# Layer 1 of a two-layer diffusion backbone: some tiles of the neighbourhood attention move to a pool at the other end of SBUF

## The chip, the core and the metric

One NeuronCore of a Trainium2 chip runs the whole kernel in one launch. Its engines are TensorE (PE; its weight loads are listed as PEld), VectorE (DVE), ScalarE (ACT), GpSimd (POOL) and SyncE (SP), which here only issues DMAs. The metric is the device time of one execution in microseconds, lower is better; it is quoted as the median of several runs. A profile is one further execution, taken by the hardware profiler.

## The reference

Two layers work on 1024 latent tokens and 256 context tokens of width 1024. Layer 0 is two kinds of grouped attention. Layer 1, which the change touches, has a convolution branch and a neighbourhood attention over a 16 by 64 grid, in which every query sees the 256 context tokens and a window of 8 by 16 grid places with a bias from a table:

```python
def odd_mixer(h_lat, h_ctx, w_in, w_out, dw_w, dw_b, ln_g, ln_b, rpb, update_ctx):
    ...
    cv, cgl, cg, dq, dk, dv, dg = split_cols(h_lat @ w_in, ODD_WIDTHS)
    x_cv, x_cgl, x_cg, x_dq, x_dk, x_dv, x_dg = split_cols(h_ctx @ w_in, ODD_WIDTHS)
    ...
    oc = conformer_conv(cv, cgl, cg, dw_w, dw_b, ln_g, ln_b)
    ...
    def d_row(args):
        r, qr = args
        rs = jnp.clip(r - kh // 2, 0, rows - kh)
        kr = lax.dynamic_slice_in_dim(k_grid, rs, kh, axis=1).reshape(bsz, kh * GRID_W, D_HEADS, HEAD_DIM)
        ...
        bias = rpb[:, dr_idx][:, :, dc_idx] + col_mask[None, None]
        ...
        return gqa_attend(qr[:, :, :, None, :], kk, vv, bias).reshape(bsz, GRID_W, D_W)
    ...
    y_lat = jnp.concatenate([oc, od * jax.nn.silu(dg)], axis=-1) @ w_out
```

`conformer_conv` is a convolution over 31 tokens in each channel, a layer norm, a SiLU and a gate; `gqa_attend` is a softmax of the scaled and biased scores times the values. All is float32.

## The kernel before

**Precision.** Every product of two float32 operands is made of three matmuls (L334 to L336) on a high and a low part: `split` (L312) rounds to the high part on ScalarE (L314, a cast) and subtracts on VectorE or GpSimd (L317) for the low part. Names ending in h or H are high, those in l or L low.

**Scheduling.** The program is written out step by step, and a scheduler that simulates the engines at build time decides the order in which each engine, and each DMA queue, gets its instructions. Tiles come from pools. A pool that opens where a closed pool lay makes each of its tiles wait for the last users of the old tiles in the same bytes (`reuse_waits="tile"`). Nearly all DMAs are issued from SP, in order: one that waits holds those behind it.

**Layer 1 in order.** Pool `cu` holds uc and gc, the convolution's output and gate (two tiles of 128 x 4 x 1024). Pool `cv` (L1224) holds the convolution's tiles; in it run the convolution's projections, its 31 taps on VectorE, ScalarE and GpSimd, and `d_proj(0)`, the attention's projections for heads 0 and 1. Then pool `ln` (L1244) holds the tiles of the layer norm, which runs in two halves of 512 tokens (`ln_steps`, L1124 to L1143: VectorE for the most part, with stores of Oc at L1143) beside `d_proj(1)`. Then `cu` closes, and two pools open: `d0` (L1261) with yo and the probability tiles ph, pl, pf, and `d1` (L1265) with the keys, values and bias tables. The attention's main loop then runs woven with `d_proj(2)`, `d_proj(3)` and the output projection.

**d_proj(i)** computes queries, keys, values and gates of two heads as sums over eight pieces of the contraction (its weights come in four loads, wr, cast to wh and wl), splits them (spq L1153 and L1155, spk, spv) and stores them in DRAM as QD, KD, VD and GD. In the order rows below, p_2723 and p_2736 are the query projections of `d_proj(2)` for the two halves of the tokens, p_2756 and p_2790 its key projections.

**The attention** works in 16 groups, one for each head and half of the grid's columns. A group needs:
- KA: the high and low part of the head's keys, 64 partitions each, loaded by L391 and L392 (two buffers), and KB, a copy of the high part by ScalarE (L397) with four rows of ones by GpSimd (L386).
- QH and QL, the queries, in pool `kv1`, loaded long before.
- a row maximum for each of four blocks of 128 queries (`maxes`, L1318): matmuls of QH with KA into the banks mx (L1326 for the context, two blocks in a bank; L1334 for the window, 440 or 320 keys), reduced by VectorE (L1328; L1335 adds the bias table bm on the way and takes an accumulator read as a second instruction). bm is loaded by L1293, three tables in a group, into two buffers.
- nmt (L418), its transpose trn (L439) and from it the last rows of QL (L440).
- for each of seven tiles: scores st (L511 from KA and QH, L515 from KB and QL), the bias bs added by VectorE (L520; loaded by L1303), the exponential (L521, L523), its split ph and pl, and the product with the values (L462 to L464; V is loaded by L1316 and has ones set by L381).

The banks mx are two, so a maximum's matmul waits for the reduction of the one two before it. The first two groups are prepared ahead of the first tile. A step of the fill (`d_proj(2)`) is held behind the sixth last L511, so the fill cannot run far ahead of the attention.

Of the kernel before, what the change touches and what calls it, by code (L numbers as in the profile page):

```python
# [10 lines left out]
F32 = mybir.dt.float32  # L11
F32R = mybir.dt.float32r
# [6 lines left out]
P = 128  # L19
# [16 lines left out]
BMB = 2  # L36
# [52 lines left out]
def tile_kernel(ctx: ExitStack, tc: tile.TileContext, a, out):  # L89
# [22 lines left out]
    def nm(s):  # L112
        uid[0] += 1
        return f"{s}_{uid[0]}"
# [263 lines left out]
    def v_tiles(pool, n, bufs=1):  # L378
        Vs[:] = [pool.tile([P, n, 192], F32R, tag="V", name=nm("Vt"), bufs=bufs) for _ in range(bufs)]
        for V in Vs:  # L380
            GP.memset(V[:, :, 128:192].bitcast(F32), 1.0)  # L381

    def k_tiles(pool, n, bufs=1):
        KB = pool.tile([P, n * P], F32R, tag="KB", name=nm("KBt"), bufs=bufs)
        KA = pool.tile([P, n * P], F32R, tag="KA", name=nm("KAt"), bufs=bufs)
        GP.memset(KB[64:68, :].bitcast(F32), 1.0)  # L386
        Ks.append((KA, KB))

# [645 lines left out]
    with ExitStack() as l1x:  # L1034
# [189 lines left out]
        with tc.tile_pool(name="cv", bufs=1, reuse_waits="tile") as vp:  # L1224
            stg[0] = vp
            taps = const("taps", [P, 4, 31], SY, vp)
            Us = []

            def convs():
                for i in range(4):  # L1230
                    while len(Us) <= i:
                        yield
                    yield from conv_steps(vp, i, Us[i])
            bg = convs()
            for i in range(4):
                U = vp.tile([P, NLAT + 30], F32, tag="U", name=nm("U"), bufs=4)
                for _ in conv_proj(vp, i, U):
                    pump(2)
                Us.append(U)
            for _ in d_proj(0):  # L1240
                pump(1)
            for _ in bg:
                pass
        with tc.tile_pool(name="ln", bufs=1, reuse_waits="tile") as vp:  # L1244
            stg[0] = vp
            lnbh = vp.tile([P, 4], F32, tag="lnbh", name="lnbh")
            VE.tensor_scalar(lnbh, lnb, 0.5, None, op0=ALU.mult)
            ones5 = vp.tile([P, P], F32, tag="ones5", name="ones5")
            VE.memset(ones5, 1.0 / 512.0)

            def lns():
                for c in range(2):
                    yield from ln_steps(vp, c)
            bg = lns()
            for _ in d_proj(1):
                pump(1)
            for _ in bg:
                pass
# [5 lines left out]
        dlow.tile([P, 48], F32, tag="pad", name="pad")  # L1264
        dpool = l1x.enter_context(tc.tile_pool(name="d1", bufs=1, reuse_waits="tile"))  # L1265
        for _ in range(2):
            k_tiles(dpool, 12, 2)
        v_tiles(dpool, 7, 2)
        od = [None, None]

        def load_head(hd):
# [4 lines left out]
        def group1(gi, hd, hf):  # L1276
            i, e = divmod(hd, 2)
            ds = slice(e * 64, (e + 1) * 64)
            bms, bss = {}, {}
# [9 lines left out]

            def load_bm(b):  # L1290
                n = (KROWS[b][1] - KROWS[b][0]) * NW
                bms[b] = dpool.tile([P, 440], F32, tag="bm", name=nm("bm"), bufs=BMB)[:, :n]
                SY.dma_start(bms[b], a["d_bm"][hd, hf, :, BMO[b] : BMO[b] + n])  # L1293
                if b == 1:
                    bms[2] = bms[1]

            def ahead(t):
                if g.tiles[t][3] is not None:
                    n = g.tiles[t][2]
                    t -= 1  # L1300
                    w = dpool.tile([P, 512 if n > 352 else 352], F32, tag="bsl" if n > 352 else "bss", name=nm("bs"),
                                   bufs=1 if n > 352 else 4)
                    SY.dma_start(w[:, :n], a["d_bs"][hd, hf, :, BSO[t] : BSO[t] + n])  # L1303
                    bss[t] = w[:, :n]
# [324 lines left out]
```

## Time and profile before

| | |
|---|---|
| time, three runs | 1554.67 us median, 1553.38 to 1559.51 |
| profiled execution, its own time | 1557.54 us |
| its span (first to last instruction) | 1555.8 us |
| mean granted TensorE clock | 0.959 of full speed |
| mean DMA traffic over the span | 128 GB/s |

Three kinds of rows are shown. A row of the timeline has the start in us from the span's start, the length in us, engine, line, operation, out<-in, and the number of instructions merged; in brackets stands how long the engine was idle before it, and what it waited for. A row of stretches has start and end, the length, the busy time of PE, PEld, DVE, ACT and POOL (with instruction counts), the granted TensorE clock as a share of full speed, the mean share in which the 16 DMA engines were busy, and GB/s. A row of the chain of waits has start, length and what held the end at that time. A row of DMA issues has out<-in, the queue, the count, KB each and the median us from issue to landing. Matmuls are pipelined: a 128 x 512 one is listed with about 0.39 us, while the next starts 0.23 us later.

### The profile page before, as it was taken

The page shows a single profiled execution, that of the slowest core. Times are in us where ns is not written, and L with a number is a line of the kernel's source. Part 1 is how long each engine was busy: PE and PEld are TensorE (multiplying, and loading weights), DVE is VectorE, ACT ScalarE, POOL GpSimd, SP SyncE. Part 2 cuts the span into 40 slices and gives each one's busy share as a digit, 9 for nine tenths or more (in the row PEclk, how much of TensorE's full clock was granted, in tenths as well). Part 3 has the DMA queues.
Part 4 walks back from the last instruction along what each step waited for, and adds up shares of the span by engine and source line. Part 5 has one row for each costly group of instructions (what it writes and reads, how often), then busy time and mean ns, then how long its engine had stood idle before and what let it go on. Part 6 is the DMA issues. An engine that isn't in the chain of part 4 may idle for free.

```text
span 1555.8 us, 21467 instructions
## 1 busy us (share of the span) xinstructions
PE 1462.5 (94%) x7084; PEld 1177.6 (76%) x7084; DVE 1046.0 (67%) x2113; ACT 747.6 (48%) x1418; POOL 800.2 (51%) x637
## 2 busy tenths in 40 slices
PE   6899999998998999999999889999999799989995
PEld 2776888896896778886877568888887688878874
DVE  2832466579678855567677848999756566577766
ACT  3721434444434564447656565443434455455562
POOL 3430334446455766557646665665632334364674
PEclk7899999999999999999999799999999899999996
DMA  9474315423312245121202021211446777877632
GB/s 365 150 247 136 102 61 174 149 65 98 114 55 77 86 145 196 45 79 43 58 28 80 23 65 60 60 48 41 152 158 212 208 220 234 257 231 230 191 86 108
DMA packets 154168, 199.83 MB, mean 128 GB/s; under 512 B 14716, under 2 KB 95816, under 8 KB 154056
## 3 DMA queue, kind: packets, MB, share of 16 engines
q1 hardware_dynamic: 147392, 186.88, 38.0%
q10 hardware_dynamic: 6664, 11.57, 2.2%
q8 instruction: 56, 0.92, 0.3%
q14 instruction: 56, 0.46, 0.1%
HBM read 148.07 MB, written 49.02 MB: 127 GB/s over the span
## 4 chain that ended last, share of the span: by engine, by line
PE 81%; DVE 11%; DMA 3%; issue 2%; ACT 2%; POOL 1%; SPq 0%; DVEq 0%; POOLq 0%; ACTq 0%
PE p L334 7%; PE p L336 7%; PE p L335 7%; PE ov L462 5%; PE ov L464 5%; PE ov L463 4%; PE st L511 4%; PE st L515 4%; PE po L334 4%; PE po L335 4%; PE po L336 4%; PE pq L334 3%; PE pq L335 3%; PE pq L336 3%; PE pg L334 2%
## 5 line engine op out<-in xcount | busy, mean ns | idle before, releaser
L317 POOL TENSOR_TENSOR pl<-pf,ph 128x512 fp32r<-128x512 f32 (+4 forms) x321 | 395.6, 1243 | 381.8 <-ACT ph L314 332.8
L523 ACT ACTIVATE pf<-st 128x512 f32<-128x512 f32 x284 | 166.2, 596 | 214.0 <-PE st L515 175.6
L317 POOL TENSOR_TENSOR wl<-wr,wh 128x512 fp32r<-128x512 f32 (+2 forms) x131 | 170.4, 1312 | 138.6 <-ACT wh L314 123.7
L314 ACT CAST ph<-pf 128x512 fp32r<-128x512 f32 (+4 forms) x364 | 209.3, 588 | 28.4 <-PE ov L463 16.3
L334 PE MATMUL p<-hh,wh 128*128 128x512 f32 x448 | 176.7, 395 | 3.0 <-DVE spv L317 1.4
L335 PE MATMUL p<-hl,wh 128*128 128x512 f32 x448 | 174.3, 390 | 0.0
L336 PE MATMUL p<-hh,wl 128*128 128x512 f32 x448 | 172.3, 390 | 0.0
L511 PE MATMUL st<-QH,KAt 128*128 128x512 f32 (+4 forms) x364 | 142.0, 391 | 7.5 <-ACT pf L523 6.7
L462 PE MATMUL ov<-ph,Vt 128*128 128x512 f32 (+4 forms) x364 | 143.3, 394 | 3.1 <-DVE y L672 2.0
L464 PE MATMUL ov<-pl,Vt 128*128 128x512 f32 (+4 forms) x364 | 142.4, 391 | 2.1 <-POOL pl L317 2.0
L463 PE MATMUL ov<-ph,Vt 128*64 128x512 f32 (+4 forms) x364 | 141.0, 387 | 0.0
L515 PE MATMUL st<-QL,KBt 68*128 68x512 f32 (+4 forms) x364 | 137.3, 388 | 2.0 <-DVE QL L440 1.9
L1099 DVE SCALAR_TENSOR_TENSOR cps<-U,taps,cps 128x512 f32<-128x512 f32 x184 | 126.0, 752 | 0.7
L314 ACT CAST wh<-wr 128x512 fp32r<-128x512 f32 (+2 forms) x134 | 81.0, 613 | 91.4 <-DMA wr<-in_od_d_dram 18.4
L334 PEld LDWEIGHTS p<-hh,wh 128*128 128x128 f32 x448 | 84.2, 188 | 21.8 <-ACT wh L314 1.9
L635 DVE TENSOR_REDUCE mp<-mx 128x1 f32<-128x512 f32 x128 | 85.3, 682 | 19.4 <-PE mx L634 18.5
L336 PEld LDWEIGHTS p<-hh,wl 128*128 128x128 f32 x448 | 84.2, 188 | 17.5
L335 PEld LDWEIGHTS p<-hl,wh 128*128 128x128 f32 x448 | 84.2, 188 | 16.8 <-issue 0.5
L334 PE MATMUL pq<-wh,hh 128*128 128x384 f32 x256 | 88.0, 344 | 2.8 <-ACT hh L314 2.8
L511 PEld LDWEIGHTS st<-QH,KAt 128*128 128x128 f32 x364 | 70.1, 193 | 24.9 <-ACT pf L523 9.9
L464 PEld LDWEIGHTS ov<-pl,Vt 128*128 128x128 f32 x364 | 71.0, 195 | 23.3 <-POOL pl L317 5.0
L956 DVE SCALAR_TENSOR_TENSOR x<-po,modT,x 128x512 f32<-128x512 f32 (+1 forms) x72 | 47.0, 658 | 61.0 <-PE po L336 60.5
(280 smaller groups left out, 3491.9 us busy)
## 6 DMA issues: line engine op xcount, KB each, us to landing
mw<-in_mod_w_dram SPq DMA_DIRECT2D x16, 1024.0 KB, 5.4
Q<-qs SPq DMA_DIRECT2D x40, 256.0 KB, 2.1
QH<-Q SPq DMA_DIRECT2D x80, 128.0 KB, 2.7
mw<-in_mod_w_dram SPq DMA_DIRECT2D x16, 512.0 KB, 6.9
wr<-in_od_d_dram SPq DMA_DIRECT2D x32, 256.0 KB, 3.1
wr<-in_ev_qkv_dram SPq DMA_DIRECT2D x16, 384.0 KB, 5.2
KAt<-KD SPq DMA_DIRECT2D x16, 384.0 KB, 5.9
wr<-in_od_wo_dram SPq DMA_DIRECT2D x22, 256.0 KB, 3.2
```

The lines of the kernel that those rows point to most:

```text
L314: acts.append(SC.copy(hi, src))
L317: (GP if leng == "g" else VE).tensor_tensor(lo, src, hi.bitcast(F32), op=ALU.subtract)
L334: PE.matmul(o, lh, rh, start=first, stop=False)
L335: PE.matmul(o, lh, rl, start=False, stop=False)
L336: last.append(PE.matmul(o, ll, rh, start=False, stop=end))
L462: PE.matmul(o, V[:, 64:192], ph[:, :n], start=(t == 0), stop=False)
L463: PE.matmul(g.ov[0:64, q0 : q0 + n], V[:, 0:64], ph[:, :n], start=False, stop=False)
L464: PE.matmul(o, V[:, 64:192], pl[:, :n], start=False, stop=(last and g.sink is None))
L511: sts.append(PE.matmul(st[:, :n], KA[:, cs], g.QH[:, q0 : q0 + n], start=True, stop=False))
L515: PE.matmul(st[:, :n], KB[0:68, cs], g.QL[0:68, q0 : q0 + n], start=False, stop=True)
L523: acts.append(SC.activation(pf[:, :n], st[:, :n], AF.Exp, scale=1.0 if g.bias else SCALE))
L1099: VE.scalar_tensor_tensor(pc, uc, w, pc, op0=ALU.mult, op1=ALU.add)
```

## The change

A pool `dh` is opened from the other end of SBUF (`side="right"`) right behind the convolution's pool, ahead of the layer norm's. The tiles KA, V, bm and bs, with the same sizes and numbers of buffers as before, are allocated in it instead of in `d1`. KB stays in `d1`, and no instruction is added or taken away.

```diff
@@ -380,9 +380,9 @@
-    def k_tiles(pool, n, bufs=1):
+    def k_tiles(pool, hi, n, bufs=1):
         KB = pool.tile([P, n * P], F32R, tag="KB", name=nm("KBt"), bufs=bufs)
-        KA = pool.tile([P, n * P], F32R, tag="KA", name=nm("KAt"), bufs=bufs)
+        KA = hi.tile([P, n * P], F32R, tag="KA", name=nm("KAt"), bufs=bufs)
@@ -1241,6 +1241,7 @@
             for _ in bg:
                 pass
+        dhi = l1x.enter_context(tc.tile_pool(name="dh", bufs=1, side="right", reuse_waits="tile"))
         with tc.tile_pool(name="ln", bufs=1, reuse_waits="tile") as vp:
@@ -1264,8 +1265,8 @@
         for _ in range(2):
-            k_tiles(dpool, 12, 2)
-        v_tiles(dpool, 7, 2)
+            k_tiles(dpool, dhi, 12, 2)
+        v_tiles(dhi, 7, 2)
@@ -1289,7 +1290,7 @@
-                bms[b] = dpool.tile([P, 440], F32, tag="bm", name=nm("bm"), bufs=BMB)[:, :n]
+                bms[b] = dhi.tile([P, 440], F32, tag="bm", name=nm("bm"), bufs=BMB)[:, :n]
@@ -1298,7 +1299,7 @@
-                    w = dpool.tile([P, 512 if n > 352 else 352], F32, tag="bsl" if n > 352 else "bss", name=nm("bs"),
+                    w = dhi.tile([P, 512 if n > 352 else 352], F32, tag="bsl" if n > 352 else "bss", name=nm("bs"),
```

Lines behind the new one have a number higher by one in the changed kernel (L1293 becomes L1294). With other waits the scheduler puts the instructions in another order, from the start of `d_proj(1)` on. Three places follow.

**SP's queue.** Before, at the end of the layer norm: stores of its output Oc and of the queries QD, and between them the loads of head 0's keys, of bm and of bs.

```order
L1143 DMA Oc<-uc 128x512 x2
L391 DMA KAt_11659<-KD_9572 64x1536
L1143 DMA Oc<-uc 128x512
L392 DMA KAt_11659<-KD_9572 64x1536
L1143 DMA Oc<-uc 128x512
L1159 DMA QD_9570<-spq_11769 128x2x256
L1293 DMA bm_11685<-in_d_bm_dram 128x440
L1159 DMA QD_9570<-spq_11769 128x2x256
L1293 DMA bm_11687<-in_d_bm_dram 128x320
L1303 DMA bs_11827<-in_d_bs_dram 128x256
```

After, these loads stand among the gate and value stores of `d_proj(0)`, ahead of the layer norm; the weights of `d_proj(1)` (its third and fourth piece) follow a few rows later, behind one more L392.

```order
L1217 DMA VD_9576<-spv_10996 128x512 x2
L391 DMA KAt_11662<-KD_9572 64x1536
L392 DMA KAt_11662<-KD_9572 64x1536
L1294 DMA bm_11688<-in_d_bm_dram 128x440
L1294 DMA bm_11690<-in_d_bm_dram 128x320
L1304 DMA bs_11830<-in_d_bs_dram 128x256
L1304 DMA bs_11832<-in_d_bs_dram 128x352
L1304 DMA bs_11834<-in_d_bs_dram 128x512
L391 DMA KAt_11665<-KD_9572 64x1536
L1198 DMA GD_9580<-sgd_11037 256x1x256
L1217 DMA VD_9576<-spv_11076 128x768
```

What moved: two of the three bm tables of group 0, three of its bs tables and three of the four halves of the keys of heads 0 and 1 went ahead by a whole `d_proj`.

**TensorE, between the key projection and the first scores.** mx_2725 to mx_2730 are the maxima of group 0, mx_2738 to mx_2743 those of group 1. Before:

```order
L336 MATMUL p_2790_11972<-hh_9483,wl_11711 128x512
L1334 MATMUL mx_2729_11755<-KAt_11659,QH_11670 128x320
L1334 MATMUL mx_2730_11758<-KAt_11659,QH_11670 128x320
L1326 MATMUL mx_2738_11792<-KAt_11659,QH_11675 128x256 x2
L1334 MATMUL mx_2739_11796<-KAt_11659,QH_11675 128x440
L1334 MATMUL mx_2740_11799<-KAt_11659,QH_11675 128x440
L1326 MATMUL mx_2741_11802<-KAt_11659,QH_11675 128x256 x2
L1334 MATMUL mx_2742_11815<-KAt_11659,QH_11675 128x320
L1334 MATMUL mx_2743_11818<-KAt_11659,QH_11675 128x320
L439 MATMUL trn_11823<-ident,nmt_11761 4x128
L515 MATMUL st_11842<-QL_11671,KBt_11658 128x512
```

After:

```order
L334 MATMUL p_2790_11975<-hh_9483,wh_11713 128x512
L1335 MATMUL mx_2740_11802<-KAt_11662,QH_11678 128x440
L335 MATMUL p_2790_11975<-hl_9484,wh_11713 128x512
L1327 MATMUL mx_2741_11805<-KAt_11662,QH_11678 128x256 x2
L336 MATMUL p_2790_11975<-hh_9483,wl_11714 128x512
L1335 MATMUL mx_2742_11818<-KAt_11662,QH_11678 128x320
L1335 MATMUL mx_2743_11821<-KAt_11662,QH_11678 128x320
L439 MATMUL trn_11826<-ident,nmt_11764 4x128
L515 MATMUL st_11845<-QL_11674,KBt_11661 128x512
L515 MATMUL st_11878<-QL_11674,KBt_11661 128x256
L439 MATMUL trn_11867<-ident,nmt_11824 4x128
```

What moved: behind the key projection's last matmul stand two maxima instead of eight. All of group 0's maxima now stand ahead of the key projections (mx_2725 to mx_2728 at the start of the query projections, mx_2729 and mx_2730 at their end), mx_2738 and mx_2739 between p_2756 and p_2790.

**VectorE, the second half of the layer norm.** uc is scaled (L1137), shifted (L1140), gated (L1141, L1142); spv and spq are splits of `d_proj(1)` and `d_proj(2)`. Before:

```order
L1137 SCALAR_TENSOR_TENSOR uc<-uc,lng,s_2667_11420 128x512 x4
L1140 TENSOR_SCALAR uc<-uc,lnb 128x512
L317 TENSOR_TENSOR spv_11636<-trv_11633,spv_11636 128x4x64
L1140 TENSOR_SCALAR uc<-uc,lnb 128x512
L1141 SCALAR_TENSOR_TENSOR uc<-thl_11602,uc 128x512
```

After:

```order
L1329 TENSOR_REDUCE mp_11734<-mx_2725_11735 128x2
L1336 ISA mx_2726_11739,mp_11734<-mx_2726_11739,bm_11688 128x440
L1336 ISA mp_11734 128x1
L1137 SCALAR_TENSOR_TENSOR uc<-uc,lng,s_2667_11423 128x512 x4
L317 TENSOR_TENSOR spv_11639<-trv_11636,spv_11639 128x4x64
L1336 ISA mx_2727_11751,mp_11734<-mx_2727_11751,bm_11688 128x440
L1336 ISA mp_11734 128x1
L1140 TENSOR_SCALAR uc<-uc,lnb 128x512
L1329 TENSOR_REDUCE mp_11734<-mx_2728_11754 128x2
L1140 TENSOR_SCALAR uc<-uc,lnb 128x512
L1141 SCALAR_TENSOR_TENSOR uc<-thl_11605,uc 128x512
```

What moved: four of group 0's reductions stand in the layer norm's second half, two ahead of L1137 and two between L1137 and L1141; before, all stood behind the query splits L1155.

## The prediction

> **What bounds the kernel now.** The page first. Its span line, its TensorE row and its chain line:
>
> ```profile
> span 1555.8 us, 21467 instructions
> PE 1462.5 (94%) x7084; PEld 1177.6 (76%) x7084; DVE 1046.0 (67%) x2113; ACT 747.6 (48%) x1418; POOL 800.2 (51%) x637
> PE 81%; DVE 11%; DMA 3%; issue 2%; ACT 2%; POOL 1%; SPq 0%; DVEq 0%; POOLq 0%; ACTq 0%
> ```
>
> TensorE is busy for 94% and holds 81% of the chain that ended last, so time can be won only where it stands still or runs at a lower clock. The table of stretches shows where that is in layer 1. Its columns: length, busy time of PE, PEld, DVE, ACT, POOL, the granted clock, the DMA share, GB/s.
>
> ```profile
> 1120.00:1140.00 20.00, 20.00 (x103) 16.68 (x102) 8.41 (x15) 7.95 (x15) 9.30 (x7) 1.00 0.49 169
> 1180.00:1210.60 30.60, 28.68 (x143) 23.07 (x141) 18.57 (x38) 10.91 (x20) 8.88 (x8) 1.00 0.82 243
> 1210.60:1222.50 11.90, 3.86 (x9) 1.94 (x10) 5.91 (x17) 0.42 (x1) 0.00 (x0) 0.60 0.79 255
> 1222.50:1226.70 4.20, 4.18 (x15) 3.79 (x16) 2.38 (x5) 2.56 (x6) 1.98 (x2) 0.51 0.26 70
> 1230.00:1360.00 130.00, 129.60 (x694) 110.46 (x692) 81.56 (x196) 68.85 (x143) 55.55 (x52) 1.00 0.78 235
> 1360.00:1364.00 4.00, 2.68 (x9) 1.54 (x10) 3.92 (x11) 2.14 (x4) 1.97 (x2) 0.89 1.06 365
> 1360.00:1380.00 20.00, 15.50 (x60) 11.56 (x61) 14.12 (x33) 11.88 (x24) 14.20 (x12) 0.83 0.91 269
> ```
>
> One hole matters: from 1210.60 to 1222.50 TensorE is busy for 3.86 of 11.90 us, and in the 4.20 us behind it the clock is 0.51. Before it (but for 1.9 us) and for 130 us behind it TensorE is full at clock 1.00, so a microsecond taken out of the hole should reach the end, unless the patch at 1360 eats it. The chain of waits (start, length, what) gives the pitch of three matmuls and names the cause; TensorE's own rows follow:
>
> ```profile
> 1208.42 0.20 PE mx L1334
> 1208.85 0.24 PE mx L1326 x2
> 1209.33 0.23 PE p L335
> ...
> 1212.05 4.51 DMA bm<-in_d_bm_dram
> ```
>
> ```profile
> 1208.26 0.36 PE L1334 MATMUL mx<-KAt,QH 128*128 128x440 f32 x1
> 1209.40 0.40 PE L336 MATMUL p<-hh,wl 128*128 128x512 f32 x1
> 1220.19 0.38 PE L439 MATMUL trn<-ident,nmt 128*4 128x128 f32 x1
> 1222.52 0.98 PE st L515 x2
> 1223.29 0.41 PE L439 MATMUL trn<-ident,nmt 128*4 128x128 f32 x1
> ```
>
> (The row of 1222.52 is the chain's, the others are TensorE's timeline.) The first two attention groups cannot start before their row maxima are known, a maximum needs its bm table, and bm has two buffers. So the third table of group 0 is a load that waits for the first table's last reader, and with it the transpose L439, QL and the first L515. On SP's queue:
>
> ```profile
> 1193.01 0.49 SPq L391 DMA_DIRECT2D KAt<-KD  x1
> 1212.05 1.74 SPq L1293 DMA_DIRECT2D bm<-in_d_bm_dram  x2
> ```
>
> The key load goes out at 1193.01 only, and the third bm at 1212.05, behind two KD stores in the order.
>
> **The change, part by part.** It adds no arithmetic. KA, V, bm and bs leave the pool that reuses the convolution's and the layer norm's space, so they no longer wait for uc and gc, only for the convolution's own tiles. Where they go out now is behind this:
>
> ```profile
> 1120.39 0.81 SPq L1217 DMA_DIRECT2D VD<-spv  x2
> ```
>
> The order shows the key loads, two bm and three bs right behind those VD stores: about 1121 instead of 1193, some 72 us early. KB, yo and the probability tiles stay where they are, and so do the memset and the copy of KB, which need the layer norm's end.
>
> *Step 1, the maxima move.* Group 0's set stands ahead of or inside d_proj(2)'s query projection, four of group 1's set inside the key projection, where TensorE is full anyway. Between the key projection's last L336 and the second L439 now stood 1223.29 − 1209.40 = 13.9 us. What is left there is a chain through VectorE, from the 440-wide matmul of the maximum `mx_2740` on:
>
> ```profile
> 1203.92 0.61 DVE L1335 CUSTOM_DVE_ANT_0 mx<-mx,bm 128x440 f32<-128x440 f32 x1
> 1204.46 0.14 DVE L1335 DVE_READ_ACCUMULATOR2_ANT mp<- 128x1 f32 x1
> 1209.20 0.69 DVE L1328 TENSOR_REDUCE mp<-mx 128x2 f32<-128x512 f32 x1
> 1210.40 0.49 DVE L317 TENSOR_TENSOR spk<-p,spk 128x320 fp32r<-128x320 f32 x1
> 1216.69 0.50 DVE L1335 CUSTOM_DVE_ANT_0 mx<-mx,bm 128x320 f32<-128x320 f32 x1 [4.47 <-DMA bm<-in_d_bm_dram]
> 1217.28 0.16 DVE L418 TENSOR_REDUCE nmt<-mp 128x4 fp32r<-128x8 f32 x1
> 1221.69 0.68 DVE L440 TENSOR_TENSOR QL<-trn,k_bd 4x512 fp32r<-4x512 f32 x1
> ```
>
> In the changed order: matmul 0.36, L1335 at 440 with its accumulator 0.75, L1328 0.69, L1335 at 320 0.64, spk 0.49 (the first L439, 0.38, runs beside it), L440 0.68, L1335 0.64, the second spk 0.49, L418 0.16: together 4.9 us. The last L336 stands some 0.7 us behind the chain's start (a 440-wide maximum, a projection matmul and two 256-wide ones), which leaves 4.2. I add 0.5 for the handovers, which the chain's pieces show at 0.03 to 0.14 us each: 4.7 us. **Saved here: 13.9 − 4.7 = 9.2 us.**
>
> *Step 2, what VectorE gets in exchange.* The maxima now stand in the layer norm's tail:
>
> ```profile
> 1184.58 2.74 DVE L1137 SCALAR_TENSOR_TENSOR uc<-uc,lng,s 128x512 f32<-128x512 f32 x4 [2.65 <-ACT s L1134]
> 1196.44 0.76 DVE L1155 SCALAR_TENSOR_TENSOR spq<-p,spq 128x256 fp32r<-128x256 f32 x2 [0.68 <-ACT spq L1153]
> 1189.12 0.50 PE L334 MATMUL p<-hh,wh 128*128 128x512 f32 x1 [1.38 <-DVE spv L317]
> 1197.34 0.47 PE L334 MATMUL p<-hh,wh 128*128 128x512 f32 x1 [0.21 <-DVE spq L1155]
> ```
>
> Two (0.69 + 0.75) fall into the 2.65 us that VectorE waits ahead of L1137: free. Two more (1.44) stand between L1137 and L1142 and push the query split L1155, which frees the bank that the key projection waits for. The 0.68 us that L1155 waits for ScalarE absorbs part, so the key projection starts 1.44 − 0.68 = 0.8 us later. Bounds: nothing (spv now stands ahead of L1140, so the wait of 1.38 us shrinks) and 1.44 us. Behind it the key projection carries 0.9 us of maxima (two 256-wide, 0.24 a pair, and two 440-wide at 0.2, twice over) where it carried 1.2 (a pair, a 440 and an st, first of 512 and then of 256 columns), 0.35 less. **Cost: 0.4 us.**
>
> *Step 3, the clock.* After the hole 4.20 us ran at 0.51, which cost 4.20 × 0.49 = 2.1 us. About 3 us of thin work remain, so I leave this loss as it is; if the clock holds, 2.1 us more are won. The nearest row is 1360 to 1364, where TensorE was busy for 2.68 of 4.00 us; the row of its longest gap, and the stretch that followed:
>
> ```profile
> 1363.73 0.79 PE L462 MATMUL ov<-ph,Vt 128*128 128x512 f32 x1 [0.46 <-DVE yo L1351]
> 1364.00:1368.00 4.00, 4.00 (x16) 3.25 (x17) 2.63 (x8) 1.84 (x5) 2.69 (x3) 0.68 1.09 350
> ```
>
> A clock of 0.68 after gaps of at most 0.46 us speaks for a drop. The Trainium skill, "TensorE: Matmul & The Clock Gate", section "HAM oscillation — how this bites in real kernels", puts the limit at idle gaps of about 3.4 us. By that rule no gap of the changed order is long enough and the clock would hold; the row above does not agree with it.
>
> *Step 4, the loads that come early.* 72 us earlier they meet the weights of d_proj(1), pieces 2 and 3 of four, on the same queue:
>
> ```profile
> KAt<-KD SPq DMA_DIRECT2D x16, 384.0 KB, 5.9
> 1132.20 0.62 ACT L314 CAST wh<-wr 128x512 fp32r<-128x512 f32 x1 [0.91 <-DMA wr<-in_od_d_dram]
> 1127.66 1.02 PE L1120 MATMUL mu<-s,ones 128*128 128x512 f32 x2
> 1205.00:1210.00 5.00, 5.00 (x25) 3.92 (x23) 1.74 (x5) 0.53 (x2) 0.00 (x0) 1.00 1.06 209
> ```
>
> Ahead of piece 2 stand four key halves of 384 KB, bm of 220 and 160 KB and bs of 128, 176 and 256 KB (128 partitions by the width in the order by 4 bytes): 2.5 MB. At 209 GB/s, the slowest stretch above with the DMA full, that is 12 us from 1121, so piece 2 lands near 1135 instead of 1132. Until it is needed TensorE has four projections on the first two pieces, 48 matmuls at the pitch of 0.23 = 11 us from 1127.66, to about 1139; with cast and split some 2 us are to spare. Cost nothing, hidden under the matmuls; without that cover each microsecond of landing beyond 1137 costs one. V's memset comes ahead of a layer-norm sum on GpSimd and costs nothing either: TensorE has the same matmuls to do meanwhile. What SP now waits for, a bm behind an L1335 at about 1189, holds back one weight load that is not needed before d_proj(2)'s second half, and the Oc stores.
>
> *Sum.* 9.2 − 0.4 = 8.8 us. Against the profiled execution, 1557.54 us (span 1555.8), that is 1548.7; it was 2.9 us above the median of the runs, and against the median 1554.67 I forecast **1545.9 us**.
>
> **Rivals.**
> *Given back at 1360.* There TensorE lost 4.5 us idle and 15.5 × 0.17 = 2.6 us of clock, with the DMA share above 1 and a query load that came late:
>
> ```profile
> 1372.92 0.47 PE L1326 MATMUL mx<-KAt,QH 128*128 128x256 f32 x2 [3.19 <-DMA QH<-QD]
> ```
>
> For it: the order of SP and VectorE is reshuffled in that region, and loads there compete. Against: what asks for those loads moves with TensorE, and a DMA share of 0.78 over the 130 us before is no limit. Half as much loss again is 3.5 us, 1549.4; twice the loss 1553. The other way, half of it gone, 1542.4.
> *The clock holds* (step 3): 1543.8.
> *No early start*: if the right-hand tiles still waited for the layer norm, the loads would go out at 1193 as now: 1554.7. The moved rows speak against it.
> *Slower*: step 4 without cover. The place is piece 2 of d_proj(1). The first 2.1 us of lateness beyond 1135 are free, the next 8.8 eat the gain, and from a landing at about 1146 on the kernel is slower: 2.7 MB in 25 us, 110 GB/s. At 85 GB/s piece 2 lands at 1153, a stall of 16 us: 1562. No stretch above with the DMA near full is under 209.
>
> **How the numbers follow.** Chances: the forecast 0.45 (1544.5 to 1547.5), the clock holds 0.13, a shorter patch at 1360 0.08, given back 0.25, no early start 0.04, slower 0.05. The bounds of step 2 (0 to 1.44) and of the handovers (0.2 to 1.5) move the gain between 7.2 and 9.9. The range goes from the shorter patch with good bounds, 1541, to the patch's loss nearly doubled, 1552.5. Half a percent, about what can be told from no change here, is 7.8 us: 1546.9. A quarter of the forecast's chance lies beyond it: faster 0.56, same 0.37, slower 0.07 (the rival and a worse patch).
>
> **What would show it.** KAt issued near 1121; PE full from 1120 to 1180; the first pair of L515 within 4 us of the key projection's last L336 (13.1 before), at about 1213; no bm load on the chain; the granted clock in the 4 us behind it; the patch at 1360 about 9 us earlier and as long. I am wrong if weight casts of d_proj(1) wait longer for wr, if the key projection waits over 1.5 us for L1155, or if KB's copy comes after 1210 and holds the first L515.

## The result and the profile after

| | before | after |
|---|---|---|
| time, median of 22 runs each on one chip | 1556.46 us (1551.0 to 1563.46) | 1549.51 us (1545.16 to 1557.62) |
| after / before | | 0.9955, 95% interval 0.9944 to 0.9967 |
| profiled execution, its own time | 1557.54 us | 1551.08 us |
| its span | 1555.8 us | 1549.3 us |
| mean granted TensorE clock | 0.959 | 0.970 |

The change wins 6.95 us, 0.45%. The forecast was 8.8 us. First the page of the changed kernel: span, TensorE's row, the chain by engine.

```profile
span 1549.3 us, 21465 instructions
PE 1454.9 (94%) x7084; PEld 1172.1 (76%) x7084; DVE 1045.0 (67%) x2113; ACT 747.3 (48%) x1418; POOL 801.2 (52%) x637
PE 77%; DVE 12%; DMA 4%; issue 3%; POOL 2%; ACT 2%; SPq 0%; DVEq 0%; POOLq 0%; ACTq 0%
```

The same 7084 matmuls; TensorE's busy time is 7.6 us shorter, which goes with the higher mean clock. Now the stretches shown of before, in the changed kernel (length, busy time of PE, PEld, DVE, ACT, POOL, granted clock, DMA share, GB/s).

```profile
1120.00:1140.00 20.00, 20.00 (x104) 16.71 (x103) 7.48 (x15) 8.28 (x15) 8.44 (x8) 1.00 0.99 283
1140.00:1180.00 40.00, 40.00 (x204) 33.64 (x202) 24.23 (x41) 15.57 (x31) 13.32 (x8) 1.00 0.53 178
1180.00:1210.60 30.60, 27.52 (x140) 22.82 (x140) 22.21 (x44) 9.73 (x17) 8.80 (x7) 1.00 0.53 179
1210.60:1222.50 11.90, 10.09 (x49) 8.03 (x48) 8.35 (x21) 6.46 (x12) 5.00 (x5) 0.86 0.57 174
1222.50:1226.70 4.20, 4.20 (x28) 3.78 (x27) 3.17 (x6) 3.38 (x9) 3.60 (x4) 1.00 0.69 185
1360.00:1380.00 20.00, 15.78 (x69) 11.89 (x68) 15.05 (x35) 11.49 (x21) 11.67 (x11) 0.91 0.77 189
1216.60:1220.00 3.40, 3.40 (x14) 3.00 (x13) 2.18 (x4) 2.24 (x6) 2.78 (x3) 0.50 0.69 204
```

The hole is nearly closed: 10.09 of 11.90 us busy instead of 3.86. But 1180 to 1210.60 got worse, 27.52 instead of 28.68. From 1120 to 1140 the DMA share rose from 0.49 to 0.99, and TensorE stayed full up to 1180. The patch at 1360 is still there, some 4 us of idle time. The last row is a piece of the fourth: 3.4 us at clock 0.50.

TensorE's timeline and then SP's queue show the events of the prediction (start, length, what; in brackets the idle time before and its reason):

```profile
1200.53 0.47 PE L334 MATMUL p<-hh,wh 128*128 128x512 f32 x1 [1.36 <-DVE spq L1155]
1212.25 0.40 PE L336 MATMUL p<-hh,wl 128*128 128x512 f32 x1
1214.89 0.59 PE L515 MATMUL st<-QL,KBt 68*128 68x512 f32 x2 [0.83 <-issue]
1216.15 0.27 PE L439 MATMUL trn<-ident,nmt 128*4 128x128 f32 x1 [0.68 <-DVE nmt L418]
```

```profile
1121.62 0.49 SPq L391 DMA_DIRECT2D KAt<-KD  x1
1130.22 0.54 SPq L353 DMA_DIRECT2D wr<-in_od_d_dram  x1
1133.11 0.33 SPq L353 DMA_DIRECT2D wr<-in_od_d_dram  x1
```

Between the key projection's last L336 and the second L439 now stand 1216.15 − 1212.25 = 3.9 us (13.9 before). The last L336 itself is 2.85 us later than before (1209.40).

**Four stretches.** Only starts of the same matmul in two traces can be subtracted. I cut the execution at four of them: one of the last L515 of layer 0 (910.20 before, 910.48 after), the key projection's last L336, the second L439, the first of eight L271 of the first final norm (1523.57 before), and the last group of L271 (1547.28 before).

| stretch | before | after | won |
|---|---|---|---|
| L515 of layer 0 to last L336 | 299.20 | 301.77 | −2.6 |
| last L336 to second L439 (the hole) | 13.89 | 3.90 | +10.0 |
| second L439 to first final norm | 300.27 | 302.59 | −2.3 |
| first to last final norm (the end) | 23.71 | 22.78 | +0.9 |

The sum is 6.0 us; with −0.3 for layer 0 and 0.7 won behind the last L271 it is the span's 6.5. So the hole gave more than was forecast, and two stretches gave 4.9 us of it back. How far one execution can be trusted: layer 0 is the same code, and but for the run with bm alone in the same order, in all kernels below, and that L515 came between 904.43 and 913.73. Two of them with the same order on TensorE (the change, and the one with its end ordered by hand) differ by 0.6 us in the first stretch and by 1.5 us in the third. The sum of the stretches of one execution is therefore no measure of the gain; the medians and ratios are.

### The profile page after: what moved, and what is told of

Read it like the earlier page. It is cut to its first block, busy times and chain, and to the rows that moved or that the text cites. A ratio compares the mean times of both kernels' runs of the same rounds, so it can differ in the third digit from the quotient of the medians.

```text
span 1549.3 us, 21465 instructions
## 1 busy us (share of the span) xinstructions
PE 1454.9 (94%) x7084; PEld 1172.1 (76%) x7084; DVE 1045.0 (67%) x2113; ACT 747.3 (48%) x1418; POOL 801.2 (52%) x637
## 4 chain that ended last, share of the span: by engine, by line
PE 77%; DVE 12%; DMA 4%; issue 3%; POOL 2%; ACT 2%; SPq 0%; DVEq 0%; POOLq 0%; ACTq 0%
PE p L334 6%; PE p L336 6%; PE p L335 6%; PE ov L462 4%; PE ov L464 4%; PE ov L463 4%; PE st L511 4%; PE po L334 4%; PE st L515 4%; PE po L336 4%; PE po L335 4%; PE pq L334 3%; PE pq L336 3%; PE pq L335 3%; PE pm L184 2%
## 5 line engine op out<-in xcount | busy, mean ns | idle before, releaser
L336 PE MATMUL p<-hh,wl 128*128 128x512 f32 x448 | 173.0, 391 | 0.0
L515 PE MATMUL st<-QL,KBt 68*128 68x512 f32 (+4 forms) x364 | 136.9, 387 | 0.9 <-issue 0.8
L336 PEld LDWEIGHTS p<-hh,wl 128*128 128x128 f32 x448 | 84.1, 188 | 17.5
```

The costliest lines, as they stand in the source:

```text
L336: last.append(PE.matmul(o, ll, rh, start=False, stop=end))
L515: PE.matmul(st[:, :n], KB[0:68, cs], g.QL[0:68, q0 : q0 + n], start=False, stop=True)
```

## Experiments: which tiles matter

Theory A: the gain comes from the first scores and maxima starting early, for which KA and bm are needed. Rivals: the other tiles carry part (B); the hole is merely the wait of the third bm table for one of two buffers (C). And for what was given back, theory D: the layer norm's late chain for the reciprocal deviation, with the rival E that VectorE has the same work in any order. The experiments ran on three chips, each beside its own runs of before, whose medians were 1554.91, 1554.75 and 1557.12 us. So the ratio to before, with its 95% interval, is what can be compared between kernels.

**Only KA and bm in the right pool.**

```diff
-        v_tiles(dhi, 7, 2)
+        v_tiles(dpool, 7, 2)
-                    w = dhi.tile([P, 512 if n > 352 else 352], F32, ...
+                    w = dpool.tile([P, 512 if n > 352 else 352], F32, ...
```

> The kernel after, with the values V and the score tables bs put back into the left pool; only the key tiles KA and the tables bm (the maxima's) stay in the right one. Theory A (the gain comes only from the first scores and maxima, which need KA and bm; V and bs were loaded in time before as well): the hole at 1210 to 1222 shrinks as in the changed kernel, second L439 at about 1216 on the profile (1223.29 before), time 1549.5 within 1.5, that is 5.5 to 8.5 below the kernel before. Rival B (the early V and bs take loads off SP's queue at the hole, and that is where part of the gain comes from): second L439 at 1219 or later, gain below 4.

Measured: 1541.34 us, ratio 0.9916 (0.99 to 0.9931), some 13.6 us below before: nearly twice what the whole change wins. Theory A had 5.5 to 8.5, and no theory had this. The stretches: −2.0, +11.2, +2.2, +3.0. Every one is better than with the whole change.

**Only V and bs in the right pool.** The two lines above as in the changed kernel, and `k_tiles(dpool, dpool, 12, 2)` and `bms[b] = dpool.tile(...)`.

> The complement: V and bs in the right pool, KA and bm back in the left one, so that their loads wait for the layer norm's tiles again. Theory A: nothing is gained, TensorE stands still at 1210 to 1222 as before, second L439 at 1223.3 within 1, time within 1.5 of the kernel before. Rival B (V and bs carry part): SP's queue is shorter at the hole, the last bm load lands earlier by the 6 loads that no longer stand there, second L439 2 to 5 earlier, gain 2 to 5. Slower is possible only if the six early loads cost something at 1120 to 1180, where TensorE has to show less than 20.00 of 20 busy.

Measured: 1551.48 us, 0.998 (0.9969 to 0.9991), 3.4 us. The stretches: 0.0, +3.6, −2.3, +3.0. At the hole rival B is right: the tables after the first two are issued from 1209.05 on instead of 1212.05, and 3.6 us are won. Of these 2.3 are lost again up to the first final norm, and 3.0 come from the last 25 us, behind the last tile of the attention. That end is looked at below.

**Before, with the third bm table in another ring.**

```diff
+                third = b == 3 and gi < 2
-                bms[b] = dpool.tile([P, 440], F32, tag="bm", ... bufs=BMB)[:, :n]
+                bms[b] = dpool.tile([P, 352 if third else 440], F32, tag="bss" if third else "bm",
+                                    ... bufs=4 if third else BMB)[:, :n]
```

> The kernel before, with one edit: the third bm table of the first two groups gets a buffer of the bs ring (352 wide), so that it needn't wait until the maxima have read the first table out of one of two bm buffers. Nothing is loaded early. Rival C (the hole is this wait: the load of 4.51 us at 1212.05 was issued only when the first maxima were done): it is issued with the first two, the last maximum ends 4 to 6 earlier, second L439 at about 1218, gain 4 to 6, most of what the change brought, without the new pool. Theory A (the early start of scores and maxima is what counts): the maxima end when VectorE gets to them behind the layer norm's tail and the key projection, gain 0 to 2, because the scores start no earlier and VectorE's queue is the limit.

Measured: 1553.97 us, 0.9992 (0.9978 to 1.0007): no gain that can be told from none. SP's queue and TensorE's timeline of this run:

```profile
1197.47 1.04 SPq L1295 DMA_DIRECT2D bm<-in_d_bm_dram  x2
1210.26 1.21 SPq L1295 DMA_DIRECT2D bm<-in_d_bm_dram  x2
1208.20 0.40 PE L336 MATMUL p<-hh,wl 128*128 128x512 f32 x1
1220.82 0.41 PE L439 MATMUL trn<-ident,nmt 128*4 128x128 f32 x1
```

The third table does go out some 14 us earlier (the second of the two loads at 1197.47), and last L336 to second L439 is still 12.6 us: the next group's tables wait for the same two buffers, at 1210.26. Rival C falls, and with it a sentence of the prediction: the chain "names the cause" when it shows the bm load at 1212.05. It names the last of several waits; the next one stood 1.3 us behind it.

**Only KA.** `k_tiles` as in the change, the other three back in `dpool`.

> Only the key tiles KA in the right pool; bm, V and bs in the left. GpSimd's order at the end is the good one, which by theory T gives 4.0. Theory A (the early start needs both: the scores KA, the maxima bm): the scores start early, but the maxima wait for bm, which waits for the layer norm's tiles, so the hole gives 0 to 2; with the 4.0 of the end a time 4 to 6 below the kernel before, about 1550. Rival F (early scores alone are enough, since bm lands in time for the maxima behind the layer norm): hole as in the changed kernel, 9 to 12 below before, about 1544.

Measured: 1547.01 us, 0.9954 (0.9937 to 0.9971). The stretches: −2.0, +8.7, −1.2, +3.0. Its hole, on TensorE:

```profile
1214.90 0.39 PE L336 MATMUL p<-hh,wl 128*128 128x512 f32 x1
1220.12 0.42 PE L439 MATMUL trn<-ident,nmt 128*4 128x128 f32 x1
```

5.2 us are left. bm goes out at 1198.35 here, when the layer norm's tiles are free, and it is early enough for most maxima. Theory A, which wanted both, is wrong; rival F is right that early keys alone close most of the hole, but its 9 to 12 us were 7.7.

**Only bm.** `bms[b]` as in the change, the other three back.

> Only the bm tables in the right pool; KA, V and bs in the left. Theory A, mended by the run with KA alone (KA is what the first scores wait for; bm out of the way of KA lands in time by itself): bm alone leaves the scores at 1202 and the hole as before, last L336 to second L439 13 to 14 us, and the end of the kernel in the good order gives 4: 1551 within 1.5. Rival G (bm is as good as KA: the maxima are the limit, the scores would come anyway): second L439 5 or more earlier, time 1546 or less.

Measured: 1551.48 us, 0.9965 (0.9947 to 0.9983). The stretches: +0.1, +1.3, −0.7, +3.0.

```profile
1206.71 0.40 PE L336 MATMUL p<-hh,wl 128*128 128x512 f32 x1
1219.29 0.41 PE L439 MATMUL trn<-ident,nmt 128*4 128x128 f32 x1
```

The hole is there as before, 12.6 us. So the early keys close the hole (8.7 of the 10.0 us by themselves); bm on top of them brings it from 5.2 to 2.8 us (11.2).

## Experiments: what was given back, and where

**The layer norm's chain issued earlier.**

```diff
-            bc = yield from rstd_steps(vp, [s1], 512, "st", 2.0)
+            bc = yield from early(rstd_steps(vp, [s1], 512, "st", 2.0))
```

`early` runs each step with a priority raised by 100, for both halves of the layer norm.

> The kernel after, with the priority of the layer norm's steps for the reciprocal deviation raised by 100 in the order by priority (a row of eight or so small instructions for each half; in both layers), so that on VectorE the second half's steps L264 to L249 stand ahead of the copies they were put behind, and the first group's maxima behind the layer norm's steps. Theory D (the 2.85 us that the last L336 comes later in the changed kernel are the late chain and the maxima ahead of the layer norm): key projection starts at 1198 within 0.7 (1200.53 in the changed kernel, 1197.34 before), second L439 at 1213.5 to 1215, time 1547.5 within 1, 1.5 to 3 below the changed kernel. Rival E (what the layer norm gains the maxima lose, since VectorE has the same work in all up to the second L439): key projection early as in D, second L439 at 1216 within 0.7, time 1549.5 within 1.

Measured: 1551.53 us, 0.9984 (0.9968 to 1.0), by the ratios 0.3% or some 4.5 us worse than the change. The stretches: −6.0, +10.0, −2.3, −0.9. The chain did come earlier, and neither D nor E describes what happened. The loss is ahead of the key projection:

```profile
1150.00:1160.00 10.00, 8.58 (x43) 6.45 (x41) 10.00 (x15) 4.92 (x9) 4.08 (x3) 1.00 0.54 185
1160.00:1170.00 10.00, 8.89 (x43) 7.46 (x43) 5.61 (x7) 3.13 (x6) 4.14 (x2) 1.00 0.53 185
```

TensorE, full there before and in the changed kernel, stands for 2.5 us. The list of what was waited for between 1140 and 1180 has its largest entry for TensorE's own rows at a cast of `d_proj(1)`'s weights on ScalarE, here numbered one line higher (us, times, longest):

```profile
PE p L335 <- ACT wh L315: 2.1, 1, 2.1
```

That the hurried layer norm took ScalarE away from this cast is a reading; it was not tried apart.

**V or bs?** KA and bm plus one of the two, against the run with KA and bm alone.

> KA, bm and V in the right pool, bs in the left. GpSimd's order at the end is that of the changed kernel again (four multiplies ahead of the reciprocal deviation). Theory T: 4 us of the trial with KA and bm alone (1541.3) are lost by that order and nothing else changes, 1545.5 within 1.5. Rival W (V's four early loads, 0.66 MB at 1120 to 1140 where DMA then is full, hold up the weights, and V in the right pool is what costs): 1548 or more, with second L439 2 or more later than with KA and bm alone, or TensorE below 40 of 40 at 1140 to 1180.

Measured with V: 1547.16 us, 0.9949 (0.993 to 0.9967); stretches −1.9, +9.9, −1.1, +0.9.

> KA, bm and bs in the right pool, V in the left. GpSimd's order at the end is the good one. Theory T: as with KA and bm alone, 1541.5 within 1.5. Rival W (the early loads of bs cost): 1545 or more, with the loss at the hole or at the stretch near 1360.

Measured with bs: 1541.75 us, 0.9917 (0.9896 to 0.9938); stretches −2.2, +11.8, −0.1, +3.0. So bs is neutral, and with V in the right pool some 5 us are gone (0.9949 against 0.9917, on one chip), which looks like a price of V. Rival W asked for 1548 or more, with the second L439 2 us later or an idle TensorE; theory T for 1545.5 within 1.5. The time was 1547.16, the hole longer by 1.2 us. Undecided.

**The end, ordered by hand.** In the changed kernel the final norm's last group waits on GpSimd behind four multiplies. Here they are put behind the reciprocal deviation of that group; `nrs[-1]` is GpSimd's instruction for it.

```diff
-EVS = "e1 c1 e2 f1 c2 f2".split()
+EVS = "e1 c1 e2 c2 f1 f2".split()
-                    GP.tensor_tensor(x, x, bcs, op=ALU.mult)
+                    with tc.issue_after(nrs[-1].ins):
+                        GP.tensor_tensor(x, x, bcs, op=ALU.mult)
```

> The changed kernel, with only the last stage ordered by hand: GpSimd's reciprocal deviation of the last 256 columns (L246) ahead of its four multiplies of the columns before (L1473 in the changed kernel), as the trials with KA and bm alone and with V and bs alone happen to have it; the final norm of the columns before stands behind it in the program. Up to 1541 the same kernel. Theory T (the 4.0 to 5.0 us between the last two groups of bc, 5.00 in the changed kernel and 0.99 in these two trials, are only this order on GpSimd and owe nothing to the pool): 4.0 less within 1, time about 1545.5. Rival W (these 4 us are late because of something earlier that the trials changed): within 1 of the changed kernel, 1549.5.

Measured: 1549.46 us, 0.9962 (0.9948 to 0.9976), no gain on the change; first to last final norm 22.65 us. Theory T, as put there, is wrong: GpSimd's order alone is not it. This run's end, on VectorE and GpSimd:

```profile
1536.97 0.16 DVE L266 TENSOR_SCALAR rbv<-trs 128x2 f32<-128x2 f32 x1 [1.50 <-PE trs L263]
1537.04 1.65 DVE L1478 SCALAR_TENSOR_TENSOR x<-x,fg,bc 128x256 f32<-128x256 f32 x4
1537.89 2.78 POOL L1476 TENSOR_TENSOR x<-x,bcs 128x256 f32<-128x256 f32 x4
1538.61 0.71 DVE L249 TENSOR_TENSOR nt<-nr,rbv 128x2 f32<-128x2 f32 x1
1539.35 0.65 DVE L250 SCALAR_TENSOR_TENSOR nt<-nt,nr 128x2 f32<-128x2 f32 x1
```

VectorE's own four multiplies now stand in front of the group's short steps, and these take 0.71 and 0.65 us instead of some 0.16, beside GpSimd's multiplies. The good end differs on TensorE as well. The run with V and bs alone, TensorE:

```profile
1539.95 0.99 PE L261 MATMUL trs<-ones,sq 128*128 128x2 f32 x4 [3.50 <-DVE nr L249]
1540.80 1.20 PE L271 MATMUL bc<-ident,nr 128*128 128x128 f32 x4
1542.56 1.22 PE L271 MATMUL bc<-ident,nr 128*128 128x128 f32 x4 [0.56 <-DVE nr L249]
```

and the changed kernel:

```profile
1535.72 1.23 PE L271 MATMUL bc<-ident,nr 128*128 128x128 f32 x4 [3.18 <-DVE nr L249]
1536.73 0.85 PE L261 MATMUL trs<-ones,sq 128*128 128x2 f32 x4
1541.52 1.22 PE L271 MATMUL bc<-ident,nr 128*128 128x128 f32 x4 [3.93 <-DVE nr L249]
```

In the good end the last group's sums (L261) come first, and the last L271 waits for 0.56 us instead of 3.93. First to last final norm is 20.6 to 20.7 us in all eight kernels of the table below with that order and 22.7 to 24.7 in the five others. Behind the last L271 part of this comes back: from there to the end of the span it is 8.4 to 9.2 us in the eight and 7.8 in the five (8.5 before), so the good order is worth some 0.5 to 1.5 us and not 2.1. Which of the three engines' orders decides was not tried alone.

**A nudge.** If V in the right pool has a price, it stays as long as V is there. If only the order differs, another order takes it away. This is the whole change, with the steps of `early` for one half (c == 0) only, and by 20 instead of 100.

```diff
-            bc = yield from rstd_steps(vp, [s1], 512, "st", 2.0)
+            bc = yield from (early if c == 0 else ident_)(rstd_steps(vp, [s1], 512, "st", 2.0))
```

> The changed kernel with one nudge in the order by priority: the steps for the reciprocal deviation of one of the layer norm's two halves 20 steps earlier. KA, V, bm and bs all in the right pool, and GpSimd's order at the end the good one. Theory O (the 8 us between the changed kernel and the one with KA and bm alone are a matter of the order that the builder falls into, not of where V lies or when it is loaded): the 4 us of the end at least are gained, 1545.5 within 1.5. Rival V (V in the right pool costs by its early loads or by its place): 1548 or more, as long as V is loaded at 1120 to 1140.

Measured: 1540.69 us, 0.9905 (0.9886 to 0.9924). Rival V, as it was put, falls: V is in the right pool and its loads go out from 1128.99 on, and the time is that of KA and bm alone. The stretches: −0.4, +11.7, −0.5, +3.0. Its hole:

```profile
1204.06 0.39 PE L336 MATMUL p<-hh,wl 128*128 128x512 f32 x1
1204.29 0.27 PE L439 MATMUL trn<-ident,nmt 128*4 128x128 f32 x1
1206.21 0.28 PE L439 MATMUL trn<-ident,nmt 128*4 128x128 f32 x1
```

The matmuls of all maxima of the first two groups stand ahead of the key projection's last L336. The −0.4 in the first stretch flatters this run: 0.8 us were gained between 910 and 1124 us, in code that the change does not touch. The stretch from the same six transposes (L1205 before) to the last L336 is 86.53 us, 1.3 longer than before:

```profile
1117.53:1204.06 86.53, 85.07 (x434) 71.24 (x433) 54.94 (x100) 32.72 (x60) 25.09 (x20) 1.00 0.65 204
```

**The third bm table in the bs ring, after the change.** The edit of the run on before above, in `dhi`.

> The changed kernel with the third bm table of the first two groups in the bs ring, so that it is loaded without waiting for the maxima that read the first one. Everything of the change in the right pool, GpSimd's order at the end the good one. Theory O: 4 from the end and 1 to 2 at the hole (last L336 to second L439 from 3.90 to 2.0 to 3.0, as with KA and bm alone): 1544 within 1.5. Rival V: 1547 or more, the 4 us of the end set off by the stretch near 1360.

Measured: 1544.07 us, 0.9922 (0.9901 to 0.9943), as theory O had it, but not by its steps: −0.8, +10.0, −3.9, +3.1. The hole keeps its 3.9 us; the gain is from ahead of it and from the end, and the third stretch takes 3.9 back.

**The best one.** KA, bm and bs right, V left, and the third table in the ring.

> KA, bm and bs in the right pool, V in the left, and the third bm table of the first two groups in the bs ring. Against the same without the ring (1541.75): the third table needn't wait for the first one's buffer, so the interval from the last L336 to the second L439 goes from 2.15 to 1.5 to 2.0, time 1541.5 within 1.5. If the time is above 1544, the order near 1360 or at the end has turned against it, which the differences stage by stage must show.

Measured: 1539.03 us, 0.9893 (0.9874 to 0.9912), the lowest median of all; its interval overlaps that of the nudge. The stretches: −2.1, +11.7, +0.9, +3.0. The hole is 2.15 us, the same as without the ring, so the edit's own reason is not borne out.

All of it, in us won against before by stretch of one profiled execution. The second column is the part of the first that lies behind the six transposes L1205 at 1124.13 us (before's time), up to which the instructions on TensorE are the same. The last column is the ratio to before on the same chip, as quoted above.

| kernel | to last L336 | of it from 1124 | hole | to first final norm | end | sum | ratio |
|---|---|---|---|---|---|---|---|
| the change | −2.6 | −2.5 | 10.0 | −2.3 | 0.9 | 6.0 | 0.9955 |
| the change, end by hand | −3.1 | −3.1 | 9.9 | −3.9 | 1.1 | 4.0 | 0.9962 |
| the change, chain 100 earlier | −6.0 | −5.2 | 10.0 | −2.3 | −0.9 | 0.7 | 0.9984 |
| the change, nudge of 20 | −0.4 | −1.3 | 11.7 | −0.5 | 3.0 | 13.8 | 0.9905 |
| the change, third bm in ring | −0.8 | −0.8 | 10.0 | −3.9 | 3.1 | 8.4 | 0.9922 |
| KA, bm | −2.0 | −1.4 | 11.2 | 2.2 | 3.0 | 14.4 | 0.9916 |
| KA, bm, bs | −2.2 | −1.4 | 11.8 | −0.1 | 3.0 | 12.4 | 0.9917 |
| KA, bm, bs, third bm in ring | −2.1 | −1.3 | 11.7 | 0.9 | 3.0 | 13.6 | 0.9893 |
| KA, bm, V | −1.9 | −1.0 | 9.9 | −1.1 | 0.9 | 7.9 | 0.9949 |
| KA | −2.0 | −1.3 | 8.7 | −1.2 | 3.0 | 8.6 | 0.9954 |
| bm | 0.1 | 0.0 | 1.3 | −0.7 | 3.0 | 3.6 | 0.9965 |
| V, bs | 0.0 | 0.0 | 3.6 | −2.3 | 3.0 | 4.4 | 0.998 |
| before, third bm in ring | 0.1 | 0.0 | 1.3 | −1.5 | 0.9 | 0.9 | 0.9992 |

Read by columns: the hole is closed where KA is early, and only there. What it costs ahead of the last L336 goes with KA too: from 1124 us on it is nothing in the three kernels without early keys and 0.8 to 5.2 us in the others. Between 910 and 1124 us the executions differ by chance: the granted clock is 0.5 there for one stretch of 3.41 us in the nudged run, for two or three in the others, and the same code takes 0.8 us less or 0.9 more than in before.

The columns behind the hole and the end move by 6 and by 4 us between kernels. Order alone does much of this: four kernels with all of the change's tiles in place (rows 2 to 5) differ by 3.4 and 4.0 us. But the column behind the hole is not above −0.5 in any kernel with V in the right pool, and −0.1 to 2.2 in the three with KA and bm early and V left. That V's place costs a microsecond or two there is not excluded.

## Why the prediction was right, and where not

**Sign, size, range.** Faster, as forecast, and inside the range; the gain was 6.95 instead of 8.8 us, just under the half percent that was set as what can be told. Of the 3.6 us between 1545.9 and 1549.51, 1.8 are the base: the 22 runs of before have their median at 1556.46, not at 1554.67. That the rest is small is in part luck: against the steps the profiled execution has 0.8 us more from the hole, 2.2 more cost ahead of it, 2.3 lost behind it (a rival had that), and 1.6 won at the end, which nothing had.

**Step 1 held.** Saved 10.0 instead of 9.2 us: 3.9 us are left where 4.7 were worked out. The 0.5 added for the handovers is not the whole of it: from the 440-wide matmul at 1211.58 to the second L439 at 1216.15 it is 4.57 us, less than the 4.9 of the rows alone, since the listed lengths overlap (the 440-wide L1336 starts at 1211.98 and what follows its accumulator read at 1212.52, 0.54 us where 0.75 were added). One sign was wrong: a bm load is on the chain of waits of the changed kernel.

```profile
1212.52 0.15 DVE mp L1336
1212.69 2.10 DMA bm<-in_d_bm_dram
1214.93 0.50 DVE mx L1336
```

It costs little, for VectorE worked on until 1214.78 (L440 at 1214.10, 0.68 us). The reason given for the hole, the third table's wait, was wrong as a cause: taken away alone it gave 1.3 us. What has to be early is KA.

**Step 2 is the one that failed: "Cost: 0.4 us" measured 2.6**, and 2.5 of it lie behind the six L1205 at 1124.13 us (1124.45 in the changed kernel). The stretch from there to the last L336, before and after:

```profile
1124.13:1209.40 85.27, 83.59 (x424) 69.75 (x423) 49.93 (x88) 32.73 (x60) 25.67 (x21) 1.00 0.56 182
1124.45:1212.25 87.80, 84.72 (x432) 70.97 (x431) 53.31 (x97) 32.57 (x60) 27.19 (x19) 1.00 0.62 199
```

*The part that was left out* is TensorE's own work: eight more matmuls stand in this stretch, and TensorE is busy for 1.1 us longer. They are maxima that left the hole and now stand ahead of the key projection. Step 1 put them where "TensorE is full anyway" and charged nothing; but a matmul that is put into a full stretch makes it longer by its own time. Step 2 booked only the other side of the move, the 0.35 us by which the key projection got shorter (0.34 measured).

*The waits* grew by 1.4 us, TensorE's idle time from 1.7 to 3.1. The wait for L1155 is 1.36 us instead of 0.21 (0.8 more was forecast), and the wait for spv shrank from 1.38 to 0.32 us, as the step's lower bound had it. What no step had is a wait of the second half's L271 (before, then the changed kernel):

```profile
1182.87 1.05 PE L271 MATMUL bc<-ident,nr 128*128 128x128 f32 x8
1185.13 1.16 PE L271 MATMUL bc<-ident,nr 128*128 128x128 f32 x8 [1.40 <-DVE nr L249]
```

It waits for VectorE's short steps, which began 2.3 us later, measured from layer 0, and ran beside GpSimd (the last section has the rows). From 1120 to 1180 TensorE is full in both kernels, so nothing was lost there. The nudged run has ten more matmuls in the stretch and 1.5 us of idle time: it pays 1.3 us, less than the rise in busy time of 1.5 (85.07 against 83.59). With KA alone six more stand there and it is 1.3 us too.

**Step 3 held**, by one window: 3.4 us at 0.50 cost 3.4 × 0.5 = 1.7 us, where 2.1 were left standing. The longest idle gap of TensorE between the last L336 and the drop was 0.83 us. The Trainium skill's limit of about 3.4 us ("TensorE: Matmul & The Clock Gate", "HAM oscillation — how this bites in real kernels") would have held the clock; the trace does not agree, and that rival did not come. What stood ahead of the drop is thin work, not a gap:

```profile
1213.00:1216.60 3.60, 1.85 (x9) 1.00 (x9) 3.28 (x11) 1.76 (x5) 0.00 (x0) 1.00 0.62 193
```

**Step 4 held.** KAt at 1121.62, the weights' pieces at 1130.22 and 1133.11, TensorE full from 1120 to 1180.

**The rival "given back at 1360"** came in part: 2.3 us were lost between the second L439 and the first final norm, of the 3.5 that it was priced at, and 0.9 came back at the end. Counted matmul by matmul from the second L439, the changed kernel is 0.4 us behind at 1355 (before's time) and 2.4 at 1391, so most of it lies at the patch. That the order there is drawn anew was its argument; that a new order can win as well as lose, and at other places too, was not seen. The change as it stands drew a poor order: with a nudge of 20 in one priority it is worth some 15 us (0.9905 of six runs, against 0.9955).

## What to carry to other kernels

Where a builder decides the order, a change of waits is two changes: the wait that it removes, which can be priced from the trace, and a new order of everything behind it, which here was worth from −9 to +3 us (first stretch, stretch behind the hole and end, added; one execution can shift such a sum by 1 to 2 us). Work that leaves a hole is not gone: where it lands in a full stretch it costs its own time. Try two or three neutral nudges before a change is judged by its time, and cut the traces at the same instructions to see which stretch moved. The load at the end of a chain of waits may be only the last of several; take it away alone before you call it the cause.

## What the runs showed of the hardware

**VectorE's short instructions beside GpSimd.** The timelines of VectorE and GpSimd, first of before:

```profile
1179.80 0.16 DVE L247 TENSOR_TENSOR nt<-nr,rbv 128x4 f32<-128x4 f32 x1 [1.13 <-POOL nr L246]
1179.99 0.16 DVE L248 SCALAR_TENSOR_TENSOR nt<-nt,nr 128x4 f32<-128x4 f32 x1
1181.49 2.52 POOL L317 TENSOR_TENSOR wl<-wr,wh 128x512 fp32r<-128x512 f32 x2 [1.72 <-PE p L335]
```

and of the changed kernel:

```profile
1182.41 1.25 DVE L247 TENSOR_TENSOR nt<-nr,rbv 128x4 f32<-128x4 f32 x1 [1.13 <-POOL nr L246]
1183.69 1.19 DVE L248 SCALAR_TENSOR_TENSOR nt<-nt,nr 128x4 f32<-128x4 f32 x1
1182.35 2.51 POOL L317 TENSOR_TENSOR wl<-wr,wh 128x512 fp32r<-128x512 f32 x2
```

On 4 columns VectorE took 0.16 us while GpSimd was idle, and 1.25 and 1.19 us while it ran two subtractions of 1.25 us each: each short instruction lasted about as long as one of GpSimd's. Beside GpSimd's 256-wide multiplies (2.78 us for four) the same steps, on 2 columns, took 0.65 to 0.71 us, above. Four 512-wide instructions that took 2.74 us beside a GpSimd that was idle but for the last 0.2 us (L1137 at 1184.58, in the prediction) took 4.91 us in the changed kernel, where GpSimd ran two subtractions of 1.3 us at 1188.21 and 1190.01:

```profile
1186.94 4.91 DVE L1137 SCALAR_TENSOR_TENSOR uc<-uc,lng,s 128x512 f32<-128x512 f32 x4 [0.68 <-ACT s L1134]
```

With the chain issued earlier, ahead of GpSimd's work, the short steps took 0.16 and 0.15 us. The Trainium skill, "SBUF — State Buffer", section "SBUF: two separate sides", says that the two engines share a pair of ports, locked for a whole instruction when VectorE reads two operands from SBUF; these rows agree. In the changed kernel L271 then waits 1.40 us for the last of these steps (its row above); before it did not wait.

**The clock.** The granted clock fell to 0.50 for 3.4 us without an idle gap over 0.83 us, behind 3.6 us in which TensorE was busy for half the time. In the run with KA and bm alone it did not fall at the hole:

```profile
1205.00:1210.00 5.00, 3.02 (x16) 2.16 (x14) 2.78 (x8) 1.13 (x3) 0.00 (x0) 1.00 0.76 247
```

Here 3.02 of 5.00 us were busy and the clock held. The 14 traces of this case say more. In each of them the granted clock changes between 1.00 and 0.50 only on an even grid of 3.41 us. Cut on this grid, from 10 us on, windows at full clock in which TensorE was busy for less than half were followed by one at half clock in 97 of 98 cases; at 50 to 60% busy in 43 of 88, at 60 to 80% in 53 of 319, at 80% or more in 15 of 5383. In the changed kernel the window from 1213.22 to 1216.63 was busy for 1.75 us, 51%. So the busy share of a window decides for the most part; what decides between 50 and 80% stays open.
